# A hybrid decoder layer on one core: value rows of the attention transposed on VectorE and by DMA, and a rearranged opening

## The chip, the core and the metric

The kernel runs on one core of a Trainium2 chip. Five engines work side by side, each with its own queue of instructions in order: TensorE (PE, with PEld for its weight loads), VectorE (DVE), ScalarE (ACT), GpSimd (POOL) and SyncE (SP, which only issues DMAs). ACT and POOL issue DMAs too. All DMAs run on the core's 16 DMA engines. SBUF and DRAM tiles are filled and emptied by DMA; matmuls write PSUM. The metric is the device time of one execution in microseconds; the median of several runs counts.

## The reference

One decoder layer over 1024 tokens of width 1024: two SwiGLU halves (width 2816), between them a mixer (16 heads of stick-breaking attention beside a Mamba-2 scan) and a cross-attention to 256 memory tokens, each inside RMS norms. What the change touches is the first SwiGLU half's beginning and the values of the attention:

```python
def rmsnorm(x, g):
    y = x32 * lax.rsqrt(jnp.mean(x32 * x32, axis=-1, keepdims=True) + EPS)
    return (y * g.astype(jnp.float32)).astype(x.dtype)

def swiglu(h, w_gu, w_down):
    g, u = jnp.split(h @ w_gu, 2, axis=-1)
    return (jax.nn.silu(g) * u) @ w_down

def stick_breaking_attention(q, k, v):
    """A[t,s] = beta_ts * prod_{s<j<t}(1-beta_tj), s<t."""
    ...
        z = jnp.einsum('bhtd,bhsd->bhts', qb, kb) * scale
        causal = s_idx[None, :] < t_idx[:, None]
        log_1mb = jnp.where(causal, jax.nn.log_sigmoid(-z), 0.0)
        suffix = lax.cumsum(log_1mb, axis=3, reverse=True) - log_1mb
        log_a = jnp.where(causal, jax.nn.log_sigmoid(z) + suffix, -jnp.inf)
        outs.append(jnp.einsum('bhts,bhsd->bhtd', jnp.exp(log_a), vb))
```

## The kernel before

**Numbers and layout.** Activations lie transposed: 8 row tiles of 128 channels, each cut into two halves of 512 tokens (hh = 0, 1). Each fp32 operand is split into a rounded high part (a cast on ACT) and a low part (a subtraction on DVE); a product is then three matmuls, high x high, high x low and low x high (mm3, L275). One projection of a 128-column weight onto one half is 8 x 3 = 24 matmuls of 128x512 (proj, L282).

**Order.** TensorE's order is that of the program: `_pe` (L101) chains every matmul to the one before, and sums a planner's clock. Work in `later` runs when that clock passes its due time; `pinned` (L145) places a small group at or after a clock. merge (L157) interleaves two streams in proportion to two planned lengths. The other engines take instructions by priority as their inputs come ready in the planner's view; inside `later`, or where `keep_in_program_order` is called, the order of the program is kept. Each queue then runs strictly in order.

**Opening.** run (L2250) loads the parameters on SP's queue. up_phase (L555) calls warm (14 matmuls on ones), then for i = 0, 1, 2 loads and splits a whole first-layer weight (wtile, L175: one 512 KB DMA, a cast on ACT, a subtraction on DVE) and calls begin(i): load_x(0) brings and splits the 8 row tiles of half 0, on SP's and GpSimd's queues in turn; the second step loads constants and sums the squares for the norm of half 0, pinned at 8500 and 13500; the third does the same for half 1. The norm is applied only to the products: the first PSUM banks are held until the norm's factors R are there (scaled, L655). gate and up (L887, L893) run weights 0, 1, 2 on half 0 and then on half 1, each product in one of three "mm" banks.

**Attention.** Heads go in 8 pairs p. inproj(p) (L1673) projects queries, keys and values; units(p) (L1864) computes the scores z, the sigmoids nb (ACT), a scan (DVE), transposes of the weights by TensorE, and products with V. merge runs units(p) beside inproj(p + 1) (L1939). For the values, steps (L1686) takes differences of neighbouring tokens into "dv" (128 channels by 512 tokens, two buffers); vtr (L1698), called three and six steps into the last key projection, turns dv in four 128x128 transposes on TensorE into a PSUM tile (tr_tile, shared with the transposes of the attention weights) and splits that into V. qevac and kevac send the rows of queries and keys by SP's queue.

Of the kernel before, what the change touches and what calls it, by code (L numbers as in the profile page):

```python
# [1 line left out]

# [8 lines left out]
F32 = mybir.dt.float32  # L11
# [36 lines left out]
class Kern:  # L48
# [232 lines left out]

    def proj(self, w, hh):  # L282

        wh, wl = w
        ps = self.t(self.mmp, [P, H], F32, "mm")
# [19 lines left out]

    def proj_now(self, w, hh):
        g = self.proj(w, hh)
# [247 lines left out]
    def up_phase(self, sp, sp2, wgu, gpre, act_d, bank, load, plain, sizes, rw=None, begin=None):  # L555
# [12 lines left out]
        if begin:  # L568
            x = sums(F32)
            self.F = [[x[(1, 4)[hh]][d // 2][:, d % 2] for d in range(KT)] for hh in range(2)]  # L570
            first = []
            begin(-1)
            for i in range(3):
                self.inlater = i < 2
                first.append(self.wtile(wgu[i]))
                begin(i)
                self.inlater = False
        S = {n: [(x[:, 0], x[:, 1]) for x in v] for n, v in sums(F32R).items()}
# [307 lines left out]

        def gate(w, hh):  # L887
            t, ps = ft(), self.proj_now(w, hh)
            with self.urgent():
                scaled(t, ps, hh)  # L890
            return t

        def up(f, hh, t, w):  # L893
            ps = self.proj_now(w, hh)
            with self.urgent():
                nc.vector.tensor_tensor(out=t, in0=t, in1=ps, op=ALU.mult)
            store(f, hh, t)

        if begin:
            ts = []  # L900
            for hh in range(2):
                up(0, hh, gate(first[0], hh), first[1])
                ts.append(gate(first[2], hh))
# [714 lines left out]
    def attention(self):  # L1618
        nc, ap = self.nc, self.ap
        with self.pools("at", ["o", "a"], ["w"]) as (op, sp, wsp, pp):  # L1620
# [52 lines left out]
            def inproj(p):  # L1673
# [12 lines left out]
                def steps(hh, t, before):  # L1686
# [3 lines left out]
                    with first():  # L1690
# [559 lines left out]
    def run(self):  # L2250
        nc, tc, ap = self.nc, self.tc, self.ap
        with tc.tile_pool(name="const", bufs=1) as cp, tc.tile_pool(name="state", bufs=1, reuse_waits="tile") as xp, \
# [31 lines left out]

            def load_x(hh):
                order = self.tc.keep_in_program_order
                for d in range(KT):
                    x, eng = self.F[hh][d], (nc.sync, nc.gpsimd)[d % 2 if hh == 0 else 0]
                    order(eng.dma_start(out=x, in_=ap["xT"][d, :, hh * H : (hh + 1) * H]))
                    self.scaled_split(self.XH[hh][d], self.XL[hh][d], x, self.par("ffn1_pre_g", d))  # L2290
                if hh == 0:
                    order(nc.gpsimd.tensor_copy(small[:, 4:5], self.XH[0][6][:, 0:1].bitcast(F32)))

            def warm():

                nc.scalar.activation(small[:, 3:4], self.eps, AF.Sqrt, bias=self.eps)
                ps = self.t(self.msp, [P, H], F32, "ms", bufs=1)
                for _ in range(14):
                    self.mm(ps, self.onesr, self.onesr[:, :].unsqueeze(1).to_broadcast([P, 4, P]), True, True)
                self.clock = 0.0  # L2300

            def norm_x(hh, t1, t2):
                accs = self.new_accs()
                for d in range(KT):
                    self.sumsq(accs, d, self.F[hh][d])
                self.pre(hh, accs, t1, t2)

            def begin(step):
                if step < 0:
                    warm()  # L2310
                elif step == 0:
                    load_x(0)
                elif step == 1:
                    consts()
                    norm_x(0, 8500, 13500)
                else:
                    load_x(1)
                    norm_x(1, 24000, 27500)

# [112 lines left out]
```

## Time and profile before

| | |
|---|---|
| median of 3 runs | 2592.11 us (2591.74 to 2594.81) |
| the profiled execution: its own time | 2592.94 us |
| the profiled execution: its span, first to last instruction | 2591.1 us |
| granted TensorE clock | 0.999 |
| DMA | 489.82 MB, mean 189 GB/s |
| attention, 1020 to 1460 us: PE / DVE / ACT busy | 438.58 / 326.95 / 246.66 us |
| first 20 us: PE / DVE / ACT busy | 17.11 / 13.19 / 15.25 us |

The profile is one execution; its span leaves out 1.8 us around the first and last instruction. A row of a timeline gives the start, the duration, the engine, the line, the operation, and in brackets the idle time ahead of it with what ended it. Durations of matmuls overlap, as they are pipelined: what one of them takes of the time is the distance between starts. A row of a wait table is who waited for whom, the sum in us, how often, and the longest.

### The profile page before, as it was taken

How to read it: one execution, taken by the hardware profiler on the slowest of the kernel's cores; microseconds unless marked ns; L12 is line 12 of the kernel's file. 1: busy time of each engine (PE TensorE's matmuls, PEld its weight loads, DVE VectorE, ACT ScalarE, POOL GpSimd, SP SyncE). 2: the span in 40 equal slices, each digit the busy share in tenths (PEclk: the TensorE clock that was granted, in tenths of full speed). 3: DMA queues.
4: the chain of work that ended last, by engine and by line, in shares of the span. 5: the costliest groups of instructions: out<-in, count | busy, mean ns of one | idle time of the engine just before them, and what ended most of it. 6: DMA issues, size and time to landing. Idle time of an engine off the chain costs nothing.

```text
span 2591.1 us, 36806 instructions
## 1 busy us (share of the span) xinstructions
PE 2570.7 (99%) x12850; PEld 2147.4 (83%) x12850; DVE 1990.0 (77%) x3049; ACT 1289.9 (50%) x2301; POOL 580.5 (22%) x676
## 2 busy tenths in 40 slices
PE   9999999999999999999999999999999999999999
PEld 7888888888787778888888898888878888888887
DVE  7889997779689884777777876876656888767767
ACT  7434444555356663555555563455554433333544
POOL 2555553001000001111111110111011655542000
PEclk9999999999999999999999999999999999999999
DMA  6448888655655526555554655647658453327554
GB/s 242 160 175 297 307 290 307 216 183 172 223 200 197 185 74 212 163 153 152 144 155 131 194 161 194 204 161 252 203 182 301 143 179 102 113 83 240 183 175 155
DMA packets 215530, 489.82 MB, mean 189 GB/s; under 512 B 26544, under 2 KB 35120, under 8 KB 215344
## 3 DMA queue, kind: packets, MB, share of 16 engines
q1 hardware_dynamic: 168080, 378.92, 44.8%
q0 software_dynamic: 23360, 65.03, 8.4%
q10 hardware_dynamic: 23904, 43.53, 4.5%
q8 instruction: 101, 1.65, 0.3%
q14 instruction: 85, 0.70, 0.1%
HBM read 327.46 MB, written 138.94 MB: 180 GB/s over the span
## 4 chain that ended last, share of the span: by engine, by line
PE 90%; DVE 3%; issue 1%; DMA 1%; ACT 1%; POOL 0%; DVEq 0%; ACTq 0%; POOLq 0%
PE mm L139 46%; PE dn L139 34%; PE z L139 2%; PE tr L142 2%; PE ms L142 1%; PE y L139 1%; PE ms L139 1%; PE seg L139 1%; PE st L139 0%; DMA wraw<-xs 0%; DVE hl L263 0%; DVE olo L270 0%; PE mm L142 0%; DVE xl L263 0%; DVE blk L729 0%
## 5 line engine op out<-in xcount | busy, mean ns | idle before, releaser
L139 PE MATMUL mm<-xh,whi 128*128 128x512 f32 x1312 | 519.7, 405 | 3.5 <-DVE xl L1968 1.5
L139 PE MATMUL mm<-xh,wlo 128*128 128x512 f32 x1280 | 491.4, 392 | 0.0
L139 PE MATMUL mm<-xl,whi 128*128 128x512 f32 (+1 forms) x1248 | 485.0, 389 | 0.3 <-DVE xl L270 0.3
L139 PEld LDWEIGHTS mm<-xh,whi 128*128 128x128 f32 x1312 | 246.8, 188 | 45.6 <-issue 3.9
L139 PEld LDWEIGHTS mm<-xh,wlo 128*128 128x128 f32 x1280 | 240.3, 188 | 52.5 <-DVE wlo L263 0.4
L139 PEld LDWEIGHTS mm<-xl,whi 128*128 128x128 f32 x1248 | 235.4, 189 | 33.9 <-DVE xl L270 1.1
L1795 DVE TENSOR_TENSOR_SCAN nb<-nb,begin 128x128 f32<-128x128 f32 (+7 forms) x128 | 171.6, 1351 | 43.3 <-ACT nb L1791 42.1
L1791 ACT ACTIVATE nb<-z,scale 128x128 f32<-128x128 f32 (+2 forms) x192 | 108.3, 581 | 69.7 <-PE z L139 68.7
L263 DVE TENSOR_TENSOR wlo<-wraw,whi 128x1024 fp32r<-128x1024 f32 x70 | 85.5, 1221 | 56.5 <-ACT whi L261 56.4
L261 ACT CAST whi<-wraw 128x1024 fp32r<-128x1024 f32 (+1 forms) x86 | 83.4, 970 | 82.9 <-PE mm L139 51.1
L1812 POOL DMA_DIRECT2D mix<-sq x64 | 53.0, 829 | 249.0 <-DVE sq L1810 196.8
L657 ACT ACTIVATE ft<-ft 128x512 f32<-128x512 f32 x88 | 55.5, 632 | 96.5 <-DVE ft L656 91.7
L139 PE MATMUL dn<-xh,wlo 128*128 128x512 f32 x296 | 101.1, 389 | 0.0
L760 POOL TENSOR_TENSOR wc<-raw,wraw 128x512 f32<-128x512 f32 x55 | 80.7, 1467 | 55.5 <-DVE wlo L263 23.4
L760 POOL TENSOR_TENSOR wc<-wraw,raw 128x512 f32<-128x512 f32 x56 | 78.6, 1404 | 52.2 <-DVE blk L263 16.7
L263 DVE TENSOR_TENSOR atl<-tr,ath 128x512 fp32r<-128x512 f32 (+1 forms) x105 | 66.1, 632 | 30.5 <-ACT ath L261 30.1
L857 POOL TENSOR_TENSOR ft<-ft,e 128x512 f32<-128x512 f32 x37 | 59.8, 1617 | 124.5 <-DVE e L853 56.5
L261 ACT CAST ath<-tr 128x512 fp32r<-128x512 f32 (+1 forms) x105 | 57.4, 546 | 59.3 <-PE tr L142 54.1
L139 PE MATMUL dn<-xh,blk 128*128 128x512 f32 x264 | 85.2, 389 | 0.0
L139 PE MATMUL mm<-ath,v 128*128 128x256 f32 x320 | 84.5, 286 | 0.0
L139 PE MATMUL mm<-atl,v 128*128 128x256 f32 x320 | 82.9, 281 | 0.0
L261 ACT CAST wlo<-wc 128x512 fp32r<-128x512 f32 x79 | 49.1, 621 | 68.0 <-PE dn L139 21.6
(591 smaller groups left out, 6781.0 us busy)
## 6 DMA issues: line engine op xcount, KB each, us to landing
whi<-dwhi SPq DMA_DIRECT2D x82, 512.0 KB, 3.7
wlo<-dwlo SPq DMA_DIRECT2D x82, 512.0 KB, 5.0
wraw<-in_w_gu SPq DMA_DIRECT2D x43, 512.0 KB, 4.1
dwhi<-bh SPq DMA_DIRECT2D x78, 256.0 KB, 4.2
dwlo<-bl SPq DMA_DIRECT2D x78, 256.0 KB, 4.1
raw<-in_w_gu SPq DMA_DIRECT2D x37, 512.0 KB, 4.0
wraw<-xs SPq DMA_DIRECT2D x56, 256.0 KB, 3.0
xs<-ft ACTq DMA_DIRECT2D x54, 256.0 KB, 2.8
```

Of the source, the lines that this page charges most:

```text
L139: self._pe(self.nc.tensor.matmul(out, lhsT, rhs, start=start, stop=stop, skip_group_check=self.more), cost)
L142: self._pe(self.nc.tensor.transpose(out, src, self.ident if ident is None else ident), 109.0)
L261: self.kp(self.nc.scalar.copy(hi, src))
L263: self.nc.vector.tensor_tensor(out=lo, in0=src, in1=hi.bitcast(F32), op=ALU.subtract)
L657: nc.scalar.activation(t, t, AF.Silu)
L760: inst = (nc.vector if early else nc.gpsimd).tensor_tensor(out=t, in0=a, in1=b, op=op)
L857: nc.gpsimd.tensor_tensor(out=t1, in0=t1, in1=e, op=ALU.mult)
L1791: nc.scalar.activation(nb[:, s0:s1], z[:, 0:n], AF.Sigmoid, scale=sc[:, i : i + 1])
L1795: nc.vector.tensor_tensor_scan(out=nb[:, 0:Wd][:, ::-1], data0=nb[:, 0:Wd][:, ::-1], data1=begin[:, S - Wd : S][:, ::-1], initial=0.0, op0 ...
L1812: nc.gpsimd.dma_start(out=self.mix_d[p][a * 64 : a * 64 + 64, csl], in_=o, accum_op=ALU.add)
```

## The change

In the attention, dv is transposed in place by DVE (which turns blocks of 32x32), stored to a DRAM tile, and read back by four DMAs, one for each quarter of 32 partitions, in runs of 32 floats, so that the blocks land where a whole transpose puts them. The split into V is unchanged but reads SBUF. In the opening, the first two weights come in halves whose splits stand between those of the row tiles; one half's low part is computed by GpSimd; row tiles 0, 1, 2, 4 and 6 of half 0 come by GpSimd's queue, 3, 5 and 7 by SP's; the parameters come by ACT's queue; the third weight is loaded and split inside the norm's sums; the norm of half 0 is pinned at 17500 and 20500; the two products of the first weights with half 0 take "dn" banks; the warm-up has 12 matmuls.

```diff
+            begin.warm()
+            first, raws = [], []
+            for i in range(2):
+                raws.append(self.t(self.wp, [P, KT, P], F32, "wraw", bufs=2))
+                first.append([self.t(self.wp, [P, KT, P], F32R, n, bufs=3) for n in ("whi", "wlo")])
...
+            def load_half(i, q):
+                order(nc.sync.dma_start(out=raws[i][:, q], in_=wgu[i][:, q]))
+            def split_half(i, q):
+                hi, lo = (x[:, q] for x in first[i])
+                order(nc.scalar.copy(hi, raws[i][:, q]))
+                eng = nc.gpsimd if i == 0 and q is halves[1] else nc.vector
+                order(eng.tensor_tensor(out=lo, in0=raws[i][:, q], in1=hi.bitcast(F32), op=ALU.subtract))
+            for q in halves:
+                load_half(0, q)
+            for d in range(KT):
+                begin.load(0, d, nc.sync if d in (3, 5, 7) else nc.gpsimd)
+            for q in halves:
+                load_half(1, q)
+            self.inlater = True
+            begin.split(0, 0)
+            split_half(0, halves[0])
+            begin.split(0, 1)
+            split_half(0, halves[1])
+            for d in range(2, KT):
+                begin.split(0, d)
+            begin.behind()
+            for q in halves:
+                split_half(1, q)
+            begin.consts()
+            begin.norm(0, 17500, 20500, lambda: first.append(self.wtile(wgu[2])))
+            self.inlater = False
+            for d in range(KT):
+                begin.load(1, d, nc.sync)
+                begin.split(1, d)
+            begin.norm(1, 24000, 27500)
...
+        def early_bank():
+            return self.t(self.dnp, [P, H], F32, "dn", bufs=4)
...
-                up(0, hh, gate(first[0], hh), first[1])
+                ps = [None if hh else early_bank() for _ in range(2)]
+                up(0, hh, gate(first[0], hh, ps[0]), first[1], ps[1])
                 ts.append(gate(first[2], hh))
...
-                    return dv
-                def vtr(hh, t):
-                    ps = tr_tile([P, 4, P])
-                    for j in range(4):
-                        self.tr(ps[:, j, :], t[:, j * P : (j + 1) * P])
-                    src = ps[:, :, :].rearrange("p j (a d) -> p a j d", a=2)
+                        nc.vector.transpose(dv, dv)
+                    o = self.tc.dram_tile([P, H], F32, name=self.nm("vt"))
+                    nc.sync.dma_start(out=o, in_=dv)
+                    return o
+                def vtr(hh, o):
+                    t = self.t(sp, [P, H], F32, "dv", bufs=2)
+                    rows = o.rearrange("(c e) (j q d) -> q e j c d", c=4, q=4, d=32)
+                    for q in range(4):
+                        nc.sync.dma_start(
+                            out=t[32 * q : 32 * q + 32, :].rearrange("e (j c d) -> e j c d", j=4, c=4), in_=rows[q]
+                        )
+                    src = t[:, :].rearrange("p (j a d) -> p a j d", j=4, a=2)
...
-                self.merge(units(p), 25500 if p else 20700, inproj(p + 1), 32500)
+                self.merge(units(p), 25500 if p else 20700, inproj(p + 1), 31600)
...
-            nc.sync.dma_start(out=self.params, in_=ap["params"])
+            nc.scalar.dma_start(out=self.params, in_=ap["params"])
...
-                for _ in range(14):
+                for _ in range(12):
...
-            def norm_x(hh, t1, t2):
+            def norm_x(hh, t1, t2, between=None):
                 accs = self.new_accs()
                 for d in range(KT):
                     self.sumsq(accs, d, self.F[hh][d])
+                    if d == 2 and between:
+                        between()
                 self.pre(hh, accs, t1, t2)
```

More of the change, by code (lines that the diff above doesn't have):

```diff
@@ L1 @@
 from contextlib import ExitStack, contextmanager
+from types import SimpleNamespace
 import numpy as np
@@ L280, in mm3, with proj @@
             self.mm(ps, wl, xh, False, last and i == n - 1)
-    def proj(self, w, hh):
+    def proj(self, w, hh, ps=None):
         wh, wl = w
-        ps = self.t(self.mmp, [P, H], F32, "mm")
+        if ps is None:
+            ps = self.t(self.mmp, [P, H], F32, "mm")
         for k in range(KT):
@@ L304, in kvproj, with proj_now @@
         return ps
-    def proj_now(self, w, hh):
-        g = self.proj(w, hh)
+    def proj_now(self, w, hh, ps=None):
+        g = self.proj(w, hh, ps)
         while True:
@@ L570, in up_phase @@
             self.F = [[x[(1, 4)[hh]][d // 2][:, d % 2] for d in range(KT)] for hh in range(2)]
[L571 to L577, printed above, removed]
+            begin.warm()
[3 more added lines that the diff above has]
+                first.append([self.t(self.wp, [P, KT, P], F32R, n, bufs=3) for n in ("whi", "wlo")])
+            halves = slice(0, 4), slice(4, 8)
+            order = self.tc.keep_in_program_order
+            def load_half(i, q):
[28 more added lines that the diff above has]
+            begin.norm(1, 24000, 27500)
         S = {n: [(x[:, 0], x[:, 1]) for x in v] for n, v in sums(F32R).items()}
@@ L885, in up_phase, with gate @@
                 at(u + d * n, soon if begin and k < 2 else now, f)
-        def gate(w, hh):
-            t, ps = ft(), self.proj_now(w, hh)
+        def early_bank():
+            return self.t(self.dnp, [P, H], F32, "dn", bufs=4)
+        def gate(w, hh, ps=None):
+            t, ps = ft(), self.proj_now(w, hh, ps)
             with self.urgent():
@@ L891, in gate, with up @@
             return t
-        def up(f, hh, t, w):
-            ps = self.proj_now(w, hh)
+        def up(f, hh, t, w, ps=None):
+            ps = self.proj_now(w, hh, ps)
             with self.urgent():
@@ L2283, in consts, with load_x, split_x, behind @@
                     nc.vector.tensor_scalar(out=g, in0=g, scalar1=0.5, scalar2=None, op0=ALU.mult)
[L2285 to L2292, printed above, removed]
+            order = self.tc.keep_in_program_order
+            def load_x(hh, d, eng):
+                order(eng.dma_start(out=self.F[hh][d], in_=ap["xT"][d, :, hh * H : (hh + 1) * H]))
+            def split_x(hh, d):
+                self.scaled_split(self.XH[hh][d], self.XL[hh][d], self.F[hh][d], self.par("ffn1_pre_g", d))
+            def behind():
+                order(nc.gpsimd.tensor_copy(small[:, 4:5], self.XH[0][6][:, 0:1].bitcast(F32)))
             def warm():
@@ L2305, in norm_x @@
                     self.sumsq(accs, d, self.F[hh][d])
+                    if d == 2 and between:
+                        between()
                 self.pre(hh, accs, t1, t2)
[L2308 to L2318, printed above, removed]
+            begin = SimpleNamespace(
+                warm=warm, load=load_x, split=split_x, behind=behind, consts=consts, norm=norm_x,
+            )
             self.kv_d = [[tc.dram_tile([P, 4, MEM], F32R, name=f"kv{h}{n}") for n in range(2)] for h in range(4)]
```

## The prediction

> **What bounds the kernel now.** I read the page first (busy time, chain of waits), then a table of busy time by stage, then TensorE's waits inside attention, then the order of time around the two places that change.
>
> ```profile
> PE 2570.7 (99%) x12850; PEld 2147.4 (83%) x12850; DVE 1990.0 (77%) x3049; ACT 1289.9 (50%) x2301; POOL 580.5 (22%) x676
> PE 90%; DVE 3%; issue 1%; DMA 1%; ACT 1%; POOL 0%; DVEq 0%; ACTq 0%; POOLq 0%
> 1020.00:1460.00 440.00, 438.58 (x2536) 380.15 (x2535) 326.95 (x454) 246.66 (x503) 67.92 (x168) 1.00 0.56 156
> PE tr L142 <- DVE v L263: 0.9, 1, 0.9
> PE ms L142 <- DVE v L263: 0.3, 1, 0.3
> PE z L139 <- DMA k<-xl: 0.2, 1, 0.2
> ```
>
> The first line is busy time by engine, the second the chain that ended last by engine, the third the attention stage (length, then PE, PEld, DVE, ACT, POOL busy, clock, DMA share, GB/s). The last three are all of TensorE's waits in attention. TensorE is busy 438.6 of 440 us and waits 1.4 us; DVE, ACT and the DMA engines (0.56) have room. So an instruction taken off TensorE here shortens the kernel by its spacing, as long as nothing new ends later than TensorE.
>
> **Attention, what goes.** Eight head pairs, two halves, four transposes each: 64 TensorE transposes.
>
> ```profile
> L142 PE MATMUL tr<-ident,dv x44: 270/272/274, 1030.8 to 1445.3; 128*128 128x128 f32 x44
> L142 PE MATMUL ms<-ident,dv x20: 270/272/303, 1203.7 to 1452.4; 128*128 128x128 f32 x20
> 1023.81 0.39 PE L139 MATMUL mm<-xh,wlo 128*128 128x512 f32 x1
> 1030.61 0.39 PE L139 MATMUL mm<-xh,wlo 128*128 128x512 f32 x1
> 1030.84 0.60 PE L142 MATMUL tr<-ident,dv 128*128 128x128 f32 x4
> 1031.51 0.40 PE L139 MATMUL mm<-xl,whi 128*128 128x512 f32 x1
> ```
>
> Durations overlap, so I take spacings. From 1023.81 to 1030.61 lie 30 matmul steps: 0.227 us each. From 1030.61 to 1031.51 lie two steps and one group of four transposes: 0.90 - 0.45 = 0.45 us for the group. 16 groups: **-7.2 us** (64 transposes). The two waits on "v" are waits for a PSUM buffer that the split of the value rows holds; after the change that split reads SBUF and holds none: **-1.2 us**. The planner's 32500 becomes 31600, as it counted 8 x 109 for these transposes in each pair; I give that nothing.
>
> **Attention, what comes.** Per half: one DVE transpose of 128x512, one store of 256 KB to a DRAM tile, and four loads of 64 KB in runs of 32 floats (128 bytes, 512 runs each, 2048 per half). All five go on SP's queue; ACT's and DVE's split stays, from SBUF instead of PSUM.
>
> ```profile
> L1691 DVE TENSOR_TENSOR dv<-ev x16: 684/691/693, 1024.3 to 1442.3; 128x511 f32<-128x511 f32 x16
> q1 hardware_dynamic: 144, 0.52, 30.9%
> q1 hardware_dynamic: 672, 0.79, 50.3%
> L1911 SPq DMA_DIRECT2D kv<-vo x8: 524/524/600, 1519.5 to 1549.9; - x8
> mix<-ev SPq DMA_DIRECT2D x16, 256.0 KB, 2.8
> ```
>
> No DVE transpose is in the trace. The nearest row is the subtraction beside it, 0.69 us for as many elements; I bound it by 0.4 and 2.8 (one to four passes) and take 0.7: 16 x 0.7 = 11 us on an engine that idles 113 of the 440 us. It costs nothing while that idle time covers it; queued behind it on DVE are "atl", the scans and "ev", which TensorE has not had to wait for. If it took 2.8 us (45 us in all), DVE would still be under its span.
>
> The two q1 lines are SP's queue in two windows of 5.0 us: packets, MB, share of 16 engines. The first holds one plain 512 KB load (128 packets of 4 KB plus 16 that signal): 0.309 x 80 = 24.7 engine-us, 193 ns a packet. The second holds such a load and one store "kv" in 512 runs of 512 bytes: 40.2 - 24.7 = 15.5 engine-us, 30 ns a packet. A straight line through both gives 14 ns at 128 bytes; as dear as a run of 512 bytes, it is 30. I take 16: a half costs 2048 x 16 / 16 = 2.0 us of all engines (3.8 at 30), so 16 halves take 33 to 61 us of a 440 us stage that uses 0.56. The store "kv" issued in 0.52 us, so four loads keep SP some 2.1 us. SP now also waits: for DVE's transpose ahead of the store, and for the store to land (2.8 us, as "mix") ahead of the loads. Behind these waits on SP stand the next weight's two loads and the key rows; weights are fetched one ahead, so only the key rows can be late.
>
> The Trainium skill speaks against this: DMA: Bandwidth & Descriptors, section Specifications, asks for 512 bytes or more per transfer, as anything shorter becomes a read-modify-write. No run here has such a transfer; the rival "dear packets" below prices it.
>
> Most halves have time: rows of a later pair are wanted long after they are sent.
>
> ```profile
> 1092.95 2.47 SPq L1671 DMA_DIRECT2D k<-xl  x4
> 1105.15 0.28 PE L139 MATMUL z<-k,q 128*128 128x256 f32 x1
> DMA  0878889973000008699979770369998899898100
> 1029.71 0.32 SPq L1688 DMA_DIRECT2D mix<-ev  x1
> 1037.45 2.48 SPq L1671 DMA_DIRECT2D k<-xl  x4
> 1041.05 0.35 PE L139 MATMUL z<-k,q 128*128 128x256 f32 x1 [0.24 <-DMA k<-xl]
> ```
>
> For the second pair the last key rows leave at 1093 and are first read at 1105. The first pair is the exception: sent at 1037.45, awaited at 1041.05. The slices (1020 to 1045, 0.625 us each) show the DMA engines empty at 1026.3-1029.4 and for about 1 us at 1035, full around. The new traffic lies ahead of these key rows on the same queue: half 0 (some 1 us of it falls into the first gap), the store of half 1 after "mix" (0.8 us), half 1's loads. With 2.0 us per half: 1.0 + 0.8 + 2.0, less about 1.8 us of room at 1035 and in the slices of 7 tenths, gives 2.0 us later; TensorE arrives 0.9 us sooner (two groups). **+3.0 us**, once (0 if all of it fits, 7 at 30 ns).
>
> **Opening.** Params go to ACT's queue, the first weight comes as two 256 KB halves first on SP, row tiles 0, 1, 2, 4, 6 on GpSimd's queue and 3, 5, 7 on SP, then the second weight in halves, constants and third weight; warm-up drops from 14 to 12 matmuls; a half of the first weight's low part is GpSimd's; the first half's two products take spare "dn" banks; the norm's pins move from 8500/13500 to 17500/20500.
>
> ```profile
> L261 ACT CAST wlo<-wc 128x512 fp32r<-128x512 f32 x79 | 49.1, 621 | 68.0 <-PE dn L139 21.6
> L263 DVE TENSOR_TENSOR wlo<-wraw,whi 128x1024 fp32r<-128x1024 f32 x70 | 85.5, 1221 | 56.5 <-ACT whi L261 56.4
> q0 software_dynamic: 3, 0.01, 3.9%
> S<-in_xT POOLq DMA_DIRECT2D x1, 256.0 KB, 4.9
> 6.83 2.57 ACT L268 ACTIVATE xh<-S,params 128x512 fp32r<-128x512 f32 x4 [0.50 <-DMA S<-in_xT]
> 7.61 0.50 PE L139 MATMUL mm<-xh,whi 128*128 128x512 f32 x1 [1.46 <-ACT xh L268]
> 9.95 2.56 ACT L268 ACTIVATE xh<-S,params 128x512 fp32r<-128x512 f32 x4 [0.54 <-DMA S<-in_xT]
> 10.70 2.74 DVE L270 SCALAR_TENSOR_TENSOR xl<-S,params,xh 128x512 fp32r<-128x512 f32 x4 [0.37 <-ACT xh L268]
> 14.18 0.39 PE L139 MATMUL mm<-xh,whi 128*128 128x512 f32 x1
> 23.43 1.02 PE L139 MATMUL ms<-small,acc 128*128 128x1 f32 x8 [0.20 <-DVE acc L362]
> 28.22 0.50 PE L139 MATMUL mm<-xh,whi 128*128 128x512 f32 x1 [0.47 <-DVE ft L656]
> ```
>
> GpSimd's queue (q0) had moved 3 packets by 4.0 us, and its first load, issued at 1.39, landed 4.9 us on, at 6.3. Tile 0 on that queue therefore comes at 6.3, against 6.8. ACT then does eight roundings of 0.64 and, between them, two half casts of 0.62: 6.3 + 6.4 = 12.7, against 9.95 + 2.56 = 12.5. TensorE's first product (24 matmuls, 7.61 to 14.18, ideally 5.4 us) ends behind the last "xl", 13.44; that stays where it is. So the first product gains nothing: **0** (-0.5 if the earlier tile 0 carries through, +0.5 by the next paragraph). What goes are two waits: 0.20 for the norm's sums, which the later pins pass, and 0.47 for a PSUM bank, which the spare banks replace; each also restarts the stream, 0.1 us or so (0.50 against 0.39). **-0.9 us**. Two warm-up matmuls fewer lengthen the 1.46 us of idle time ahead of the first matmul by some 0.5; nothing hangs on them unless the granted clock falls there. Behind that the second half's tiles come next; their loads queue behind the third weight, but 72 matmul steps cover them.
>
> One piece speaks against: a half split on GpSimd while DVE is the pace.
>
> ```profile
> 76.52 1.78 POOL L760 TENSOR_TENSOR wc<-raw,wraw 128x512 f32<-128x512 f32 x1
> 77.08 1.78 DVE L729 SCALAR_TENSOR_TENSOR braw<-braw,params,braw 128x512 f32<-128x512 f32 x1
> 83.33 0.75 DVE L729 SCALAR_TENSOR_TENSOR rpost<-rpost,params,dg 128x512 f32<-128x512 f32 x1 [1.96 <-ACT dg L676]
> ```
>
> Beside a GpSimd operation the same DVE instruction took 1.78 us, alone 0.75: 1.0 us more, less the 0.6 that DVE is spared (half of 1.22), and the 0.1 of ACT: that is the +0.5. The Trainium skill, Advanced Engine Details and Errata, section GPSIMD Details, says that the two share a read and a write interface and collide when DVE has two SBUF inputs; the trace agrees (1.78 against 0.75).
>
> **Sum**, against the profiled execution (2592.94 us, span 2591.1): -7.2 - 1.2 + 3.0 - 0.9 = -6.3, so 2586.6. The median of the runs shown, 2592.11, is 0.83 lower, and so is the forecast: **2585.8**. A measurement of this kernel can tell about 0.2% (5.2 us) from no change: faster is below 2586.9, slower above 2597.3.
>
> **Rivals.** (1) *All hidden*: the short runs fit into the gaps and the first pair's key rows come as now. For it: 0.56 share. Against it: the 0.24 us wait, so no slack there. -9.3: 2582.8. Chance 0.22.
>
> (2) *Dear packets*: twice the price of the 512-byte run, 60 ns. A half takes 7.7 us of all engines, 16 take 123 us, share 0.84. In the first pair half 0 fits some 2 us of its 7.7 into the first gap: 5.7 + 0.8 + 7.7 - 1.8 = 12.4 us late, and 0.9. -9.3 + 13.3 = +4.0: 2596.1, within 0.2%. Against it: the line through two rows gives a quarter. Chance 0.10. By the page's rule above (the Trainium skill, DMA: Bandwidth & Descriptors, Specifications) it would be the case to expect.
>
> (3) *The wait moves to ACT*, slower:
>
> ```profile
> ACT nb L1791 <- PE z L139: 58.2, 95, 1.7
> ACT q L268 <- DMA ev<-in_memT: 1.2, 1, 1.2
> ```
>
> The cast of the value rows waited for TensorE; now it waits for four loads, and the sigmoids "nb" are queued behind it on ACT. Scores have two PSUM banks, and ACT waits for them up to 1.7 us, so about that much lateness is free; beyond it TensorE stops for the score bank. If loads land 2.7 us behind their place in ACT's order, each of 16 halves costs 1 us: -6.3 + 16 = +9.7, 2601.8. It decides from 1.7 us. For it: four issues of 0.52 us and a queue full of weights. Against it: the other cast of freshly loaded data waited 1.2 us and cost TensorE nothing. Chance 0.15.
>
> (4) *Not what it says*: the opening gains nothing as GpSimd's queue starts late; that is inside the forecast's own range.
>
> **How the numbers follow.** Forecast 0.53, own range 2582 to 2591 (stall 0 to 7, opening +0.5 to -1.4). The range takes in (1) with the opening at its best and (2), and leaves out (3): 2580.5 to 2596.5. Faster: 0.64 of the forecast and all of (1), 0.56; slower: (3), 0.15; the rest 0.29.
>
> **What would show it.** Right: no transposes from "dv" on PE; matmul steps of 0.227 where groups stood; a DVE transpose near 0.7 us; one wait of a few us on "k<-xl" near 1040; first product's end near 14 us. Wrong: ACT waiting on DMA ahead of "v" in many halves with TensorE waiting on "nb" (rival 3); short loads landing over 8 us after issue (2); a first matmul well before 7 us.

## The result, and the profile after

| | before | after |
|---|---|---|
| median of 6 runs each | 2593.46 us (2591.62 to 2595.47) | 2607.11 us (2604.60 to 2610.90) |
| ratio | | 1.0055, interval 1.0045 to 1.0065 |
| the profiled execution: time / span | 2592.94 / 2591.1 us | 2607.52 / 2605.7 us |

The change makes the kernel 0.55% slower. The forecast was 2585.8 us, its range 2580.5 to 2596.5, with a chance of 0.15 for slower by over 0.2%: wrong in sign, and outside the range.

The page after: busy time, then the chain that ended last by engine.

```profile
PE 2569.2 (99%) x12784; PEld 2145.4 (82%) x12784; DVE 2000.7 (77%) x3066; ACT 1290.2 (50%) x2303; POOL 583.1 (22%) x678
...
PE 89%; DVE 5%; DMA 3%; issue 2%; ACT 1%; POOL 0%; DVEq 0%; SPq 0%; ACTq 0%; POOLq 0%
```

TensorE is still the bound and has fewer matmuls; of the chain DVE has 5% instead of 3, and DMA 3% instead of 1. The attention stage after the change (length; PE, PEld, DVE, ACT, POOL busy; clock; DMA share; GB/s) shows no loss:

```profile
1020.00:1460.00 440.00, 439.35 (x2501) 379.45 (x2500) 333.24 (x461) 243.03 (x495) 66.87 (x167) 1.00 0.65 175
```

TensorE's longest waits of the whole run do:

```profile
PE dn L140 <- DVE e L861: 8.8, 1, 8.8
PE dn L140 <- ACT whi L586: 3.7, 1, 3.7
PE mm L140 <- ACT whi L262: 2.6, 1, 2.6
PE ms L140 <- DVE atl L264: 2.4, 1, 2.4
```

Before, the longest single wait was 1.5 us. Where they fall in time is seen by pairing the matmuls of two traces in order and taking the start in the one less the start in the other. This table is worked out that way against the profiled execution of the kernel before (median of the pairs within 2.5 us of the time named, which is the time in the kernel before; + is late; between 1043 and 1451 us the kernels with the new value rows run some matmuls in another order, so the end of attention is read at 1452, where the order is the same again):

```
                 20     46     89    113    1031   1452   1462   1515   1562   2580
after           +5.7   +5.7   +5.7  +15.5  +13.0   +4.7   +6.8  +10.8  +12.7  +14.5
values          +0.0   +0.0   +0.0   +0.1   -1.7  -10.2   -6.5   -2.3   -2.2   -1.5
opening         +5.1   +6.2   +6.2  +15.9  +14.3  +14.4  +14.4  +14.4  +16.5  +16.4
order           +6.2   +7.7   +7.7   +9.0  +10.7   +2.4   +4.5   +8.7   +9.0   +9.8
low on DVE      +1.4   +0.7   +0.7   +3.5   +2.1   -6.2   -2.5   +1.7   +1.8   +2.8
order+buffer    +2.9   +2.1   +2.1   +3.3   +3.2   -5.4   -3.3   +0.8   +2.9   +4.8
values+turn     +1.3   +0.9   +0.9   +0.9   -1.1   -9.7   -6.0   -6.0   -5.8   -5.1
 +splits        +1.8   +1.4   +1.4   +1.6   -0.4   -9.0   -8.9   -8.9   -8.8   -7.9
 +banks         +0.5   -0.2   -0.2   -0.2   -2.3  -10.8  -10.8  -10.8  -10.1   -9.6
all put right   +3.6   +2.8   +2.8   +3.9   +5.9   -2.2   -2.1   -2.2   -1.3   -1.0
splits alone    -0.2   -0.2   -0.2   -0.2   -2.0   -1.5   -1.5   -1.5   -1.0   -1.0
```

The rows below the first are the experiments: values and opening are experiment 1, order 2, low on DVE 3, order+buffer 4, values+turn 7, +splits and splits alone 8, +banks and all put right 9; experiments 5 and 6 have no row. Single profiles drift by 1 to 2 us in stretches with the same code (the last row is -2.0 at 1031, long before its edit acts), so a change of several us along a row counts, not its level. In the first row there are four: +5.7 in the opening, +10 near 100 us, -8 in attention, as forecast, and +8 at the end of attention.

**Opening.** The timeline of the kernel after:

```profile
7.93 0.72 ACT L269 ACTIVATE xh<-S,params 128x512 fp32r<-128x512 f32 x1 [5.15 <-DMA S<-in_xT]
...
8.56 0.60 ACT L586 CAST whi<-wraw 128x512 fp32r<-128x512 f32 x1
...
9.21 0.80 PE L140 MATMUL dn<-xh,whi 128*128 128x512 f32 x1 [3.72 <-ACT whi L586]
...
16.95 0.33 SPq L186 DMA_DIRECT2D wraw<-in_w_gu  x1
...
24.39 1.04 ACT L262 CAST whi<-wraw 128x1024 fp32r<-128x1024 f32 x1 [7.12 <-DMA wraw<-in_w_gu]
...
25.48 0.51 PE L140 MATMUL mm<-xh,whi 128*128 128x512 f32 x1 [2.57 <-ACT whi L262]
```

Tile 0 landed at 7.9 us; before, it was 6.8, and the forecast was 6.3. The first product starts at 9.21 instead of 7.61: 1.1 us of that is the tile, the other 0.5 the cast of the first weight's half, which had landed near 4.0 us but stands behind the rounding of tile 0 in the order of the changed code. Its first twelve matmuls then start 0.43 us apart instead of the usual 0.23, and so it ends 3.1 us late (the next product starts at 17.31 instead of 14.18). The third weight's load is issued at 16.95; before, at 7.62:

```profile
7.62 0.33 SPq L185 DMA_DIRECT2D wraw<-in_w_gu  x1
```

Its first product then waits 2.57 us. The granted clock falls, in the opening and where TensorE has waited (window, its length, busy time of PE, PEld, DVE, ACT, POOL, then the clock, the DMA share and GB/s):

```profile
0.00:10.00 10.00, 5.18 (x14) 3.80 (x14) 1.56 (x5) 3.60 (x6) 3.32 (x13) 0.88 0.79 265
10.00:20.00 10.00, 10.00 (x36) 7.66 (x35) 7.70 (x12) 7.24 (x14) 6.27 (x10) 0.78 0.60 194
...
100.00:110.00 10.00, 5.27 (x13) 4.16 (x14) 7.22 (x8) 1.76 (x3) 7.95 (x5) 0.50 0.22 76
...
1510.00:1520.00 10.00, 7.59 (x38) 6.71 (x38) 5.80 (x8) 3.38 (x6) 1.04 (x3) 0.83 0.33 98
```

Before, all these windows stand at 1.00.

**Near 100 us.** The first group of half-size products (seven, L807 before) copies two products out of PSUM on ACT (t5 and d, both shown as "sq"), subtracts them on GpSimd and adds a third on DVE (e). First the timeline before, then after:

```profile
82.09 0.59 ACT L816 COPY sq<-mm 128x512 f32<-128x512 f32 x1 [3.13 <-PE mm L139]
...
82.58 0.72 ACT L676 ACTIVATE dg<-dg,params 128x512 f32<-128x512 f32 x1
...
84.93 0.58 ACT L820 COPY sq<-mm 128x512 f32<-128x512 f32 x1
...
85.59 1.32 POOL L821 TENSOR_TENSOR sq<-sq,sq 128x512 f32<-128x512 f32 x1 [2.85 <-ACT sq L820]
...
90.51 2.97 PE L139 MATMUL dn<-S,whi 128*128 128x512 f32 x12 [0.30 <-DVE e L826]
```

```profile
87.69 0.72 ACT L711 ACTIVATE dg<-dg,params 128x512 f32<-128x512 f32 x1
...
90.49 0.73 ACT L711 ACTIVATE acc<-acc,params 128x512 f32<-128x512 f32 x1 [2.08 <-DMA acc<-in_xT]
...
94.87 0.58 ACT L851 COPY sq<-mm 128x512 f32<-128x512 f32 x1
...
98.33 0.62 ACT L262 CAST whi<-wc 128x512 fp32r<-128x512 f32 x1 [1.32 <-POOL wc L795]
...
98.85 0.58 ACT L855 COPY sq<-mm 128x512 f32<-128x512 f32 x1
...
101.73 1.71 POOL L856 TENSOR_TENSOR sq<-sq,sq 128x512 f32<-128x512 f32 x1
...
104.73 5.40 PE L140 MATMUL dn<-S,whi 128*128 128x512 f32 x12 [8.81 <-DVE e L861]
```

Before, ACT takes the first copy and then the scaling of dg. After, the copy stands behind the scalings of dg, acc and cb and behind casts, one scaling waits for a transfer and one cast for GpSimd, and the copy comes 12.8 us later than before although TensorE is only 5.7 us late. No line of that code was changed.

**Attention.** The operations that come in (a group, then the DMA issues with KB each and us to landing):

```profile
L1735 DVE STREAM_TRANSPOSE dv<-dv 128x512 f32<-128x512 f32 x16 | 11.2, 701 | 0.3
```

```profile
dv<-vt SPq DMA_DIRECT2D x64, 64.0 KB, 2.9
```

The transpose takes 0.70 us, as much as taken. The short loads land in 2.9 us. SP's queue between 1020 and 1445 us, packets, MB and share of 16 engines, first before, then after:

```profile
q1 hardware_dynamic: 26905, 58.93, 46.0%
```

```profile
q1 hardware_dynamic: 59803, 68.30, 56.0%
```

10.0% of 425 us times 16 are 680 engine-us more. Not all of it is the short runs: stores are in it, and other loads that fall into the one window and not into the other. Taken packet by packet from the trace, the 32768 packets of 128 bytes took 13.0 ns each in the mean, 425 engine-us in all; the prediction took 16. The packets of 512 bytes took 28 ns in both traces.

TensorE's only wait in this stage is for the first pair's key rows, and these are not late: they leave 12.7 us after their time in the kernel before, where TensorE is 13.0 us behind, although seven of the short loads go just ahead of them on the same queue.

```profile
1044.71 5.38 SPq L1745 DMA_DIRECT2D dv<-vt  x7
1050.14 2.56 SPq L1710 DMA_DIRECT2D k<-xl  x4
PE z L140 <- DMA k<-xl: 0.4, 1, 0.4
```

### The profile page after: what moved, and what is told of

The parts are those of the page before. It is cut to its first block, busy times and chain, and to the rows that moved or that the text cites. A ratio compares the mean times of both kernels' runs of the same rounds, so it can differ in the third digit from the quotient of the medians.

```text
span 2605.7 us, 36847 instructions
## 1 busy us (share of the span) xinstructions
PE 2569.2 (99%) x12784; PEld 2145.4 (82%) x12784; DVE 2000.7 (77%) x3066; ACT 1290.2 (50%) x2303; POOL 583.1 (22%) x678
## 3 DMA queue, kind: packets, MB, share of 16 engines
q8 instruction: 101, 1.65, 0.3%
## 4 chain that ended last, share of the span: by engine, by line
PE 89%; DVE 5%; DMA 3%; issue 2%; ACT 1%; POOL 0%; DVEq 0%; SPq 0%; ACTq 0%; POOLq 0%
PE mm L140 48%; PE dn L140 32%; PE z L140 3%; PE tr L143 2%; PE ms L140 1%; PE y L140 1%; PE ms L143 1%; PE seg L140 1%; DVE hl L264 1%; PE st L140 0%; DMA wraw<-in_w_dn 0%; DVE acc L364 0%; DMA wraw<-xs 0%; DVE F L1105 0%; DVE wlo L264 0%
## 5 line engine op out<-in xcount | busy, mean ns | idle before, releaser
L140 PE MATMUL mm<-xh,whi 128*128 128x512 f32 x1296 | 510.7, 403 | 5.5 <-ACT whi L262 2.6
L140 PE MATMUL mm<-xh,wlo 128*128 128x512 f32 x1264 | 485.7, 392 | 0.5 <-DVE wlo L264 0.5
L140 PE MATMUL dn<-xh,wlo 128*128 128x512 f32 x312 | 108.2, 392 | 0.0
L140 PE MATMUL dn<-xh,whi 128*128 128x512 f32 x256 | 90.3, 395 | 3.7 <-ACT whi L586 3.7
```

The costliest lines, as they stand in the source:

```text
L140: self._pe(self.nc.tensor.matmul(out, lhsT, rhs, start=start, stop=stop, skip_group_check=self.more), cost)
```

## The experiments

Ratios are against runs of the kernel before on the same chip, with their 95% interval.

**1. The two parts alone.** "Values" is the kernel before with this and the due time 31600; "opening" is the changed kernel without it:

```diff
+                        nc.vector.transpose(dv, dv)
+                    o = self.tc.dram_tile([P, H], F32, name=self.nm("vt"))
+                    nc.sync.dma_start(out=o, in_=dv)
...
-                    ps = tr_tile([P, 4, P])
-                    for j in range(4):
-                        self.tr(ps[:, j, :], t[:, j * P : (j + 1) * P])
```

> The kernel before with only the change to attention's value rows (VectorE transpose, one store and four short loads for each half, and the due time 31600 in place of 32500); its opening is the old one. Theory A, that the changed kernel's loss of about 14 us sits in the opening and the first 110 us and the value rows gain what they were forecast to: 2582 to 2588 us, with the delay against the kernel before falling by 7 to 9 us between 1031 and 1445 us, and about 2 to 6 us of it given back after 1450, where the changed kernel lost 6 us between 1449 and 1520. Theory B, that the short transfers also cost elsewhere (DMA share 0.65 against 0.56) and the end of attention is lost to them: 2590 to 2596 us, no faster than before.

> The kernel before with only the rearranged opening; the value rows are turned by TensorE as before, due time 32500. Theory A, the loss is the opening's alone (5.7 us by 50 us, a further 9 to 10 us at a wait for a sum on VectorE near 100 us, little given back): 2604 to 2611 us, delay +12 to +16 us from 110 us on to the end. Theory B, the changed opening would cost only the 5.7 us of the first 50 us, and the wait near 100 us belongs to something else: 2597 to 2600 us.

Values: 2591.99 us, ratio 0.9996 (0.9987 to 1.0006). Opening: 2610.16 us, 1.0064 (1.0049 to 1.0079). The opening alone costs 16.9 us, more than the whole change. Its theory A holds: the wait near 100 us (8.5 us in this run) belongs to the opening. Of the values, theory A had the gain inside attention right (-8.5 us from 1031 to 1452), but not the time, which falls into theory B's range: 8.0 us of the gain are gone again by 1562. TensorE in "values" at the end of attention:

```profile
1447.71 0.50 PE L139 MATMUL mm<-xh,whi 128*128 128x512 f32 x1 [1.12 <-ACT xh L268]
...
1448.73 0.76 PE L139 MATMUL mm<-xl,whi 128*128 128x512 f32 x1 [0.53 <-DVE xl L270]
...
1500.44 0.49 PE L142 MATMUL ms<-ident,nb 128*128 128x128 f32 x3
...
1503.33 1.17 PE L139 MATMUL ms<-ident,cmem 128*128 128x128 f32 x4 [2.41 <-DVE atl L263]
```

Two places: the output projection's first products wait for xh and xl, and the transposes of cmem wait for atl, because they write the buffer "ms" that the group just ahead of them has filled. Before, that group went to "tr":

```profile
1506.95 0.49 PE L142 MATMUL tr<-ident,nb 128*128 128x128 f32 x3
...
1507.27 0.61 PE L139 MATMUL ms<-ident,cmem 128*128 128x128 f32 x4
```

**2. The order of the copies.** The changed kernel, with ordering edges between five pairs, the first ahead of the second: the copy t5 and the scaling of dg; t5 and the cast of the fifth weight sum (w4); the copy d and the cast of the first tile of B12 (x0); d and the cast of the sixth weight sum (w5); the subtraction on GpSimd (sub) and the next group's first weight sum (p0).

```diff
+            waiting += [("t5", "dg"), ("t5", "w4"), ("d", "x0"), ("d", "w5"), ("sub", "p0")]
...
+                for pair in [p for p in waiting if p[0] in marks and p[1] in marks]:
+                    self._after(marks[pair[1]], marks[pair[0]])
```

> The changed kernel with five ordering edges and nothing else: in the first block of products, the copies of two products from PSUM on ScalarE stand ahead of the scalings of dg, acc and cb and of two casts, and the subtraction on GpSimd ahead of the next weight sum, as they stood in the kernel before. Theory A, the 8.8 us wait near 95 to 104 us (and the clock of 0.50 behind it) comes from the order in which the copies were queued on ScalarE and GpSimd: that wait falls under 1 us, the delay at 113 us is 5 to 7 us instead of 15 to 17, and the time is 2595 to 2600 us. Theory B, the wait comes from late loads of the x tiles (acc and cb landed at 90 and 91 us) or from VectorE itself: the wait stays over 4 us and the time stays at 2603 to 2609 us.

2602.68 us, ratio 1.0038 (1.0025 to 1.0051). The wait is 2.4 us, more than the 1 us of theory A but far from 8.8; the windows from 90 to 110 us stand at clock 1.00, and from 89 to 113 us the delay grows by 1.3 us instead of 9.8. So the order did cause most of it. In time the edges bring 4.4 us (2607.11 to 2602.68) and not 8.5, and theory A's range is missed by 3 us. Two things show in this profile: the opening was 2 us later (third weight: a wait of 3.6 us), and near 480 us another 3.1 us were lost, at a wait of 2.4 us for ACT's F. That place waited up to 3.2 us in the profiles with a changed opening (in experiment 5 no wait shows there), 1.0 before; why it varies was not traced.

**3. The low half on VectorE.**

```diff
-                eng = nc.gpsimd if i == 0 and q is halves[1] else nc.vector
+                eng = nc.vector
```

> The changed kernel with the low half of the first weight's second part made by VectorE instead of GpSimd. With that the third weight's load takes the buffer of the first weight instead of the second's, so it waits for VectorE's second low part (about 10.6 us) instead of the last one of the second weight (16.93 us), and the copies of the first block stand where they stood before. Theory A, the third weight's late load is worth 2.5 us of the opening's 5.7 and the order of the copies the 9 to 10 us near 100 us: the third weight's load is issued at 10.5 to 13 us, the delay at 50 us is 2.5 to 4 us, at 113 us 3 to 5 us, and the time 2592 to 2597 us. Theory B, the delay is set by the first product and the order in which x tiles land, so that the third weight comes late anyway: delay at 50 us 5 to 6 us, time 2596 to 2600 us; if the wait near 100 us stays too, 2604 to 2609 us.

2599.05 us, ratio 1.0022 (1.0012 to 1.0031), 2 us over theory A's range; it lies in that of theory B, whose delay of 5 to 6 us at 50 us did not come. The third weight's load goes at 10.23 us and nothing waits for it:

```profile
10.23 0.33 SPq L186 DMA_DIRECT2D wraw<-in_w_gu  x1
```

The delay at 46 us is 0.7 us, better than expected, since tile 0 landed at 6.25 us in this profile; then 2.8 us come in one group of products later, again behind copies on ACT and GpSimd (a wait for e of 2.1 us near 115 us). One edit of 0.68 us on VectorE moved the third weight's buffer and the order 80 us later, so this run alone separates nothing; the next does.

**4. The buffer of the third weight.** The kernel of experiment 2, and:

```diff
-            begin.norm(0, 17500, 20500, lambda: first.append(self.wtile(wgu[2])))
+            begin.norm(0, 17500, 20500, lambda: first.append(self.wtile(wgu[2], raws[0])))
...
+            if getattr(self, "third", None) is not None:
+                self._after(load.ins, self.third)
```

> The kernel with the five ordering edges, and the third weight loaded into the first weight's buffer instead of the second's (its load is traced into that buffer, and the fourth weight's load is put behind it); the low half stays on GpSimd. Theory A, the buffer chosen is what made the third weight late: its load is issued at 11.5 to 13 us (when GpSimd's low half is done) instead of 17, the wait of the third weight's first product (2.6 to 3.6 us in the three runs with the old buffer) falls under 0.5 us, the delay at 41 us is 3.5 to 5.5 us instead of 8, and the time is 2597 to 2600.5 us (2602.7 with the edges alone). Theory B, the weight lands late whenever it is issued, since what is moved from 10 to 25 us fills the transfers (share 1.0 of 16 engines): the wait stays over 2 us, time 2601 to 2604 us.

2597.37 us, ratio 1.0016 (1.0006 to 1.0025): theory A, with less delay than it gave (3.5 to 5.5 us at 41 us). The load goes at 11.62 us, the waits for the third weight (3.6 and 0.5 us in experiment 2) are gone, and the delay at 46 us is 2.1 instead of 7.7 us. What the load had waited for in the changed kernel stands among the waits of SP's queue:

```profile
SPq L186 <- DVE wlo L588: 3.3, 1, 3.3
```

DVE's last low part of the second weight ended at 16.93 us, and the load went at 16.95: it had been given the second weight's buffer, though the first's was free some 5 us sooner, when GpSimd's low half ended.

**5. The clock.** The kernel of experiment 3 with 24 warm-up products.

```diff
-                for _ in range(12):
+                for _ in range(24):
                     self.mm(ps, self.onesr, self.onesr[:, :].unsqueeze(1).to_broadcast([P, 4, P]), True, True)
```

> The changed kernel with both halves of the first weight's low part on VectorE, and 24 warm-up products in place of 12 (the kernel before has 14). Theory A, the clock of 0.85 (0.76 to 0.83 in the others) granted from 10 to 20 us comes from TensorE's idle time of 1.1 to 3.7 us between the last warm-up product and the first real one: with the gap filled the clock is 0.98 to 1.00 in that window and the delay against the kernel before at 17 us falls from +1.4 to at most +0.5 us. Theory B, the clock falls for another reason (the waits among the first products): it stays at 0.76 to 0.88 with the gap filled.

One execution, 2597.57 us. The clock is as in theory A:

```profile
0.00:10.00 10.00, 8.90 (x26) 6.85 (x26) 1.23 (x4) 3.33 (x5) 3.33 (x13) 1.00 0.78 259
10.00:20.00 10.00, 9.59 (x40) 7.06 (x40) 9.78 (x15) 10.00 (x20) 6.15 (x8) 1.00 0.90 311
```

The delay at 17 us is +2.0 us, not +0.5: tile 0 landed at 8.25 us here, and the warm-up products themselves last until 9.65. That the clock falls with the gap is shown, on this one execution; what it is worth in time is not.

**6. Tile 0 by SP's queue.** Also on the kernel of experiment 3.

```diff
-                begin.load(0, d, nc.sync if d in (3, 5, 7) else nc.gpsimd)
+                begin.load(0, d, nc.sync if d in (0, 3, 5) else nc.gpsimd)
```

> The changed kernel with both halves of the first weight's low part on VectorE, and x tiles 0, 3 and 5 loaded by SP's queue in place of 3, 5 and 7, so that tile 0 comes behind the first weight's two halves on SP. Theory A, tile 0 by GpSimd's queue is what made the first product late and unsteady (it landed at 7.9, and at 6.25 us in the run with VectorE's halves): by SP's queue it lands at 5.5 to 6.8 us, and the first product starts at 6.8 to 8.1 us, now held by tile 0 or the weight's half. Theory B, the landing is set by what all queues move in the first 8 us (DMA share 0.79) and not by the queue: tile 0 lands at 7 to 8 us from SP too.

One execution, 2596.08 us. Tile 0 came at 7.05 us:

```profile
7.05 0.72 ACT L269 ACTIVATE xh<-S,params 128x512 fp32r<-128x512 f32 x1 [4.29 <-DMA S<-in_xT]
```

By GpSimd's queue it landed between 6.25 and 8.25 us in seven profiles of the same issue (median 7.4). 7.05 is in theory B's range and among the landings by GpSimd's queue: that this queue makes the tile late is not borne out, on one execution.

**7. The turn over the transposes' buffers.** The kernel "values", and in vtr:

```diff
+                    turn[0] = (turn[0] + 1) % 3
```

> The kernel before with the value rows' change alone, and one thing more: the turn over the three PSUM buffers of the transposes (two named tr, one named ms) is advanced once for each half of the value rows, as it was when TensorE turned them, so that every transpose of the weights falls on the buffer it had before. Theory A, the 2.4 us wait of the transposes of cmem for VectorE's atl near 1503 us in the run with the values alone, and the lower clock behind it (0.83 for 10 us), come from that turn being shifted by 16 modulo 3: the wait is gone, the delay between 1490 and 1515 us no longer rises by 3 to 4 us, and the time is 2587 to 2590 us. Theory B, VectorE is late there whatever buffer is used (busy 9.9 of 10 us two windows before), so that the wait moves to the next transpose: time 2590.5 to 2593 us.

2589.70 us, ratio 0.9983 (0.9974 to 0.9992). The group ahead of cmem is on "tr" again and the wait is gone:

```profile
1500.95 0.49 PE L142 MATMUL tr<-ident,nb 128*128 128x128 f32 x3
...
1501.28 0.61 PE L139 MATMUL ms<-ident,cmem 128*128 128x128 f32 x4
```

From 1462 to 1515 us the delay stays at -6.0, where "values" lost 4.2: 2.4 us of waiting, the rest the slower clock behind it.

**8. The splits for the output projection, earlier; and whether that is a gain of its own.**

```diff
-                if n > 7:
-                    mix_split(n - 8)
+                if n > 5:
+                    mix_split(n - 6)
...
-                    if n < 2:
-                        for k in ((5, 6), (7,))[n]:
-                            mix_split(k)
+                    if n == 0:
+                        mix_split(7)
```

> As the kernel with the turn kept, and the eight splits of the mixer's rows (ScalarE xh, VectorE xl) for the output projection issued two steps of the last pair's projections earlier. Theory A, the 1.1 and 0.5 us waits of the first products of the output projection for ScalarE's sixth xh and VectorE's sixth xl near 1448 us, and the clock of 0.94 and 0.89 behind them, are the other 3 us that the values' gain gives back: these waits go and the time is 2 to 3.5 us under the kernel with the turn kept alone (2584 to 2587 us). Theory B, VectorE is full there (9.9 of 10 us) and whatever is moved ahead of the scans makes the scans late instead: within 1 us of the kernel with the turn kept.

> The kernel before with one edit: the eight splits of the mixer's rows two steps earlier, as in the best kernels; value rows turned by TensorE, old opening. It tells whether the 2585.5 us of the kernel with the values' change, the turn kept and the splits earlier is the values' gain or the splits' own. Theory A, the splits only matter once TensorE comes 8 us sooner (in the kernel before the sixth xh was ready just as its product started, with no idle time shown there): 2591.5 to 2594 us, no faster than before. Theory B, the earlier splits gain by themselves, whatever the value rows do: 2586 to 2590 us.

With the values' change and the turn: 2585.46 us, ratio 0.9970 (0.9958 to 0.9982); the same edit on the kernel before: 2593.55 us, 1.0002 (0.9993 to 1.0011). Theory A both times. Of the waits for xh and xl, one of 0.28 us is left, the clock there is 1.00, and the -9.0 us at the end of attention is still -8.8 at 1562 us. The value rows are worth some 8 us; the turn and the splits only keep them.

**9. The spare banks alone, and everything.** The first takes early_bank and its two uses from the change, on top of the kernel of experiment 8; the second is the whole change with the edits of experiments 2, 4, 7 and 8.

```diff
-                up(0, hh, gate(first[0], hh), first[1])
+                ps = [None if hh else early_bank() for _ in range(2)]
+                up(0, hh, gate(first[0], hh, ps[0]), first[1], ps[1])
```

> The kernel with the value rows' change, the turn kept and the splits two steps earlier (2585.5 us), the opening as before, and of the changed opening only the PSUM banks: the first half's first two products go to dn banks. Theory A, the 0.47 us wait of the second half's first product for VectorE's ft at 28.2 us goes, and nothing else moves: 2584.5 to 2585.5 us, the same within the measurement, and the wait is gone from the trace. Theory B, the new order of the banks makes a later wait of it, as the other edits of the opening did: 2587 to 2592 us.

> The whole change, with everything that the runs have named put right: the five ordering edges, the third weight in the first weight's buffer, the turn over the transposes' buffers kept, and the mixer's rows split two steps earlier. Theory A, the four causes add up: the kernel with the edges and the buffer, less 5 to 7 us for the end of attention: 2591 to 2595 us, the rest against the 2585.5 us of the old opening being the first product's delay and the lower clock of the first 20 us. Theory B, the causes hide one another: 2596 to 2601 us.

Banks: 2584.47 us, ratio 0.9965 (0.9953 to 0.9978), the fastest of all, though against 0.9970 no difference is shown; the wait of 0.47 us at 28 us is gone. Everything: 2589.69 us, 0.9986 (0.9977 to 0.9995), 1.3 us below theory A's range and far from B's: the causes add up, and the whole change then beats the kernel before, but not the kernel with the old opening.

## Why the prediction was wrong, by its own steps

- **Attention, what goes** (-7.2 and -1.2): right. From 1031 to 1452 us the delay falls by 8.3 us after, 8.5 in "values".
- **First pair's key rows** (+3.0): did not come. The wait for k is 0.4 us, against 0.24 before, and the rows are no later than TensorE; the range "0 to 7" held it, at its lower end. One of its terms was too dear (16 ns a run for the 13.0 measured, where the straight line through the prediction's own two rows gives 13 and not the 14 written there), but the runs did not show where the rest went. This is what rival 1 said of attention.
- **The sum took the -8.4 to the end of the kernel: this step failed in attention.** "As long as nothing new ends later than TensorE" was looked up inside 1020 to 1460 us only. Right behind it two things ended later: the splits of the mixer's rows, whose place among ACT's and DVE's work did not move up with TensorE (+3.7 in "values" from 1452 to 1462 us, 1.65 of it the two waits, with the clock at 0.94 and 0.89 around them), and the transposes of cmem, because 16 calls fewer of a turn over three buffers shift every later group by one (+4.2 up to 1515 us). Experiments 7 and 8 remove them one at a time.
- **Opening, "the first product gains nothing: 0"**: mis-sized; it ended 3.1 us late, 1.6 of it by its later start and 1.5 by its slower pace. Tile 0's landing was read from one load that came first on GpSimd's queue while SP's queue carried a tile and a whole weight; it came at 7.4 us in the median, not 6.3, and 7.9 in the profile after. The sum followed ACT to its last rounding, but not to the half cast that the first product needs. The two waits of the -0.9 did go, and the half split on GpSimd cost DVE what was feared only in part: the subtraction beside it took 1.18 us, alone 0.74.
- **"Nothing hangs on them unless the granted clock falls there"**: it fell, to 0.78 from 10 to 20 us; experiment 5 brought it back by filling the gap.
- **"Their loads queue behind the third weight, but 72 matmul steps cover them"**: true of the second half's tiles, for which TensorE never waits, but the third weight itself was left out, and this step failed. When its load would go was never worked out. Its buffer's release sets it, 16.95 us instead of 7.62; the waits for it are 2.6 and 0.5 us after, and the delay at 46 us is 5.6 us less in experiment 4 than in 2, of which 4.1 us are these waits.
- **The opening's sum ended at 28 us: the dearest step.** It priced the opening's own instructions. The other engines' order is made ahead of time from the planner's view of when inputs are ready, and a changed opening changed that order for ACT and GpSimd at 85 to 102 us: about 10 us there in both traces that have it, against a forecast of -0.9 (+0.5 at worst) for the whole opening. Experiment 2 shows the order as the cause of 8.5 of them; in its time 4.4 us came back. That the planner puts it so because TensorE is later in its view was only argued.
- **Rivals 2 and 3** fell: 13 ns a run instead of 60, and no wait of the value rows' cast for a transfer in the trace (one other cast on ACT is put down as waiting 0.6 us for such a load, and TensorE lost nothing by it). On rival 2, the Trainium skill's rule of at least 512 bytes (DMA: Bandwidth & Descriptors, Specifications) is in part borne out: a run of 128 bytes took 13 ns where one of 512 took 28, 1.9 times as much a byte; but these 425 engine-us lay in a stage with room and cost no time.
- **Rival 4**, the opening gaining nothing as GpSimd's queue starts late, was the right place, and it was held to be inside a range of +0.5 to -1.4. (The lower end of the whole range, 2580.5, does not follow from its terms, which give 2582.3; nothing hangs on it.)

What stays open: what makes tile 0's landing vary, why the wait near 480 us varies, and 1.8 us that the kernel after loses between 1562 us and the end.

## What to carry to other kernels

When work is taken off the bounding engine, follow the gain past the stage, to the first places where the engine now arrives early, and look at every buffer that is dealt out in turn: a call fewer shifts all later users. When a planner or scheduler fixes the order of the other queues, an edit at one place can move instructions at another; compare the order of the instructions on each engine before the times. And price a load from the moment its buffer comes free, not from its place in the program.

## What the runs showed of the hardware

Short waits of TensorE can cost more than themselves. After the wait of 2.41 us for atl the clock's mean was 0.83 over 10 us, which at half speed is 3.4 us of it. In the 8.8 us wait it fell, and the twelve products behind it took 5.40 us instead of 2.97. Filling the gap of the opening brought 1.00. But the length alone does not decide: the wait of 1.46 us ahead of the first product in the kernel before was followed by 1.00 and one of 1.11 us in experiment 3 by 0.85, and the wait that is left near 100 us in experiment 2 is also 2.41 us long and was followed by 1.00. What decides is not shown. The Trainium skill (TensorE: Matmul & The Clock Gate, Part 1: The HAM clock gate) puts the fall to half speed behind an idle window of about 3.4 us; half speed agrees (0.50 from 100 to 110 us), but at atl 2.41 us of waiting were enough.

A transpose of 128x512 in blocks of 32x32 took VectorE 0.70 us, as much as a subtraction of that size (0.69), and DMA loads of 64 KB in runs of 128 bytes landed in 2.0 to 4.5 us.
